# Router logits of a decoder layer: the router's columns stationary in four column groups, the tokens moving

## The chip, the cores and the metric

One core of one Trainium2 chip runs the whole layer in one launch. The metric is device time in microseconds (us), the median of several executions. The kernel before takes 634.29 us (three executions, 633.48 to 638.74).

## What is computed

A decoder layer on 512 tokens of 1024 features: an RMS norm, a combined projection, three groups of heads (differential attention, an RWKV-7 recurrence, cross-attention to a memory), an output projection, and then a mixture of 16 experts. The change lies in the step between the output projection and the experts, the router:

```python
g_logits = xt @ w_gr + b_gr                       # 512 x 4
g_idx = argmax(g_logits)                          # the group of 4 experts
e_logits = (xt @ w_er + b_er).reshape(T, 4, 4)    # 512 x 16
top_v, top_i = top_k(e_logits[rows, g_idx], 2)    # two experts of the group
gate = one_hot(...) * softmax(top_v) * softmax(g_logits)[g_idx]
for e in range(16):
    y += gate[:, e] * (silu(xt @ w_gate[e]) * (xt @ w_up[e])) @ w_down[e]
```

Here `xt` is the normalised row of a token (512 x 1024), and the two router matrices have 4 and 16 columns, kept side by side as 20 columns. The gates decide which tokens an expert gets, so no expert can start before all 512 tokens have been routed.

## The kernel before

The tokens are four tiles of 128 (t0 to t3). The output projection of a tile is made in two halves of 512 columns; the first half is done early for all four, the second half tile by tile (`out_part`, lines L998 to L1000: three float32r products per block, high and low parts of both operands). While one tile is projected, the tiles before it are routed, so that the vector and scalar engines work beside TensorE. The order in which the program names these steps is the string `ORDER`: `a` and `b` are the two quarters of a tile's projection, `x`, `l` and `s` are steps of its routing. The order on each engine is then set by a scheduler that runs a timeline of the whole program in advance and takes, for each engine, what is ready and has the highest priority. Thirty small filler products (`w30`, L1204) have the lowest priority; they stand where TensorE would have nothing else.

`route` does for one tile:

- eight transposes (L1091), four to a PSUM bank, and two ScalarE copies of the banks into `xT` (L1092), which has one buffer for all tiles;
- the logits (L1103): eight float32 products, one per 128 features, summed in PSUM. The stationary operand is a chunk of `xT` (128 features x 128 tokens), the moving one 20 columns of `wr_sb`. Each float32 product runs as two passes on the engine, so a tile has 16;
- on VectorE thirteen small operations from the scaling of the logits (`lgs`, L1105) to `member` (L1121), which marks the two experts of each token;
- one short product with a triangular matrix (L1130), and one with ones for every earlier tile (L1129), to count the members: the rank of each token in its expert (`rankm`, L1131), and a one-hot of the first expert's slots (`ohf`, L1133);
- eight float32 products with that one-hot (L1136, 16 passes) which gather the tokens of expert 0 into the PSUM tile `py`.

After the fourth tile, `py` is split into high and low parts (`xh`, L1267, ScalarE; `xl`, L1269, VectorE), and the products of expert 0 begin (L243 to L245). The weights of the experts arrive on SyncE's queue, and each block of 512 KB is split by ScalarE (`whi`, L96) and VectorE (`wlo`, L97) before it can be used.

The small PSUM tiles of the router come from a pool of two buffers, `pl`, handed out in turn as the program names them: the logits of a tile (`pr_`), then its counts (`pk`), then the next tile's logits.

Of the kernel before, what the change touches and what calls it, by code (L numbers as in the profile page):

```python
# [10 lines left out]
F32 = mybir.dt.float32  # L11
# [3 lines left out]
AF = mybir.ActivationFunctionType  # L15
# [5 lines left out]
P = 128  # L21
# [3 lines left out]
KC = D // P  # L25
# [125 lines left out]
def hybrid_layer_kernel(ctx, tc, x, mem, positions, cols, w_in, w_kv, w_out, wa2, g2, ffn, wr, br,  # L151
                        wg, wu, wd, out):
    nc = tc.nc
    V, A, G, T = nc.vector, nc.scalar, nc.gpsimd, nc.tensor
# [10 lines left out]
    pools = {"ps": psum_ctx.enter_context(tc.tile_pool(name="psa", bufs=2, space=PSUM))}  # L165
# [5 lines left out]
    def pp():  # L171
        return psp.tile([P, 512], F32, name="pp", bufs=4)
# [32 lines left out]
    ident = const.tile([P, P], F32, name="ident")  # L205
# [27 lines left out]
    bones = const.tile([P, P], F32, name="bones")  # L233
# [89 lines left out]
    wr_sb = rc.tile([P, KC, 20], F32, name="wr_sb")  # L323
# [706 lines left out]
    pools["ps"] = ctx.enter_context(tc.tile_pool(name="psl", bufs=2, space=PSUM, reuse_waits="tile"))  # L1030

    def pl(n):
        return pools["ps"].tile([P, 96], F32, name="pl", bufs=2)[:, 0:n]

    gain = rt.tile([P, D], F32, name="gain", bufs=1)
    with later():
# [31 lines left out]
    def first_max(val, mxv, oh):  # L1068
        mi = rt.tile([P, 1], F32, name="fm_i")
        V.tensor_reduce(mxv, val, axis=AX.X, op=ALU.max)  # L1070
        V.scalar_tensor_tensor(oh, val, mxv, rank4, op0=ALU.is_equal, op1=ALU.mult)
        V.tensor_reduce(mi, oh, axis=AX.X, op=ALU.max)
        V.tensor_scalar(oh, oh, mi, -BIG, op0=ALU.not_equal, op1=ALU.mult)
# [7 lines left out]
        (V if i else G).tensor_mul(xns[t][:, c0:c0 + n], x1c, gain[:, c0:c0 + n])  # L1081

    last_act = []

    def route(t, x1):
        tk = slice(t * P, (t + 1) * P)
        xT = rt.tile([P, KC, P], F32, name="xT", bufs=1)
        for b in range(2):
            ps = pp()
            for k in range(4):  # L1090
                T.transpose(ps[:, k * P:(k + 1) * P], x1[:, (b * 4 + k) * P:(b * 4 + k + 1) * P], ident)  # L1091
            last_act.append(A.activation(xT[:, b * 4:b * 4 + 4, :].rearrange("p a b -> p (a b)"), ps, AF.Copy))  # L1092
            if b == 0:
                yield
        yield
        r = rt.tile([P, 1], F32, name="rx1")
        V.tensor_reduce(r, sqs[:, t, :], axis=AX.X, op=ALU.add)
        G.tensor_scalar(r, r, 1.0 / D, RMS_EPS, op0=ALU.mult, op1=ALU.add)
        G.tensor_tensor(r, r, mhalf, op=ALU.pow)
        yield  # L1100
        pr_ = pl(32)
        for k in range(KC):
            T.matmul(pr_[:, 0:20], xT[:, k, :], wr_sb[:, k, :], start=k == 0, stop=k == KC - 1)  # L1103
        lg = lgs[:, t, :]
        V.scalar_tensor_tensor(lg, pr_[:, 0:20], r, br_sb, op0=ALU.mult, op1=ALU.add)  # L1105
        goh = rt.tile([P, 4], F32, name="goh")
        first_max(lg[:, 0:4], tops[:, 0, t:t + 1], goh)
        el = rt.tile([P, 4, 4], F32, name="el")
        V.tensor_add(el, lg[:, 4:20].rearrange("p (a b) -> p a b", a=4), goh[:, :, None].to_broadcast([P, 4, 4]))
        elf = el.rearrange("p a b -> p (a b)")  # L1110
        best = rt.tile([P, 8], F32, name="best")
        where = rt.tile([P, 8], mybir.dt.uint32, name="where")
        wheref = rt.tile([P, 2], F32, name="wheref")
        V.max(best, elf)
        V.max_index(where, best, elf)
        V.tensor_copy(wheref, where[:, 0:2])
        V.tensor_tensor(hots[:, :, t, :], iota16[:, None, :].to_broadcast([P, 2, NE]),
                        wheref[:, :, None].to_broadcast([P, 2, NE]), op=ALU.is_equal)
        V.tensor_copy(tops[:, 1:3, t], best[:, 0:2])
        oh1, oh2 = hots[:, 0, t, :], hots[:, 1, t, :]  # L1120
        V.tensor_add(member[:, t, :], oh1, oh2)  # L1121
        xn = xns[t]
        last_act.append(A.activation(xn, xn, AF.Copy, scale=r))
        nc.scalar.dma_start(xn_d[tk, :], xn)
        nc.sync.dma_start(out[tk, :], x1)
        yield
        pk = pl(32)
        for u in range(t):
            T.matmul(pk[:, 0:NE], onb, member[:, u, :], start=u == 0, stop=False)  # L1129
        T.matmul(pk[:, 0:NE], tri, member[:, t, :], start=t == 0, stop=True)  # L1130
        V.scalar_tensor_tensor(rankm[:, t, :], pk[:, 0:NE], 1.0, member[:, t, :], op0=ALU.add, op1=ALU.mult)  # L1131
        ohf = rt.tile([P, CAP], F32, name="ohf", bufs=4)
        V.tensor_scalar(ohf, slot1, rankm[:, t, 0:1], None, op0=ALU.is_equal)  # L1133
        yield
        for k in range(KC):
            T.matmul(first_py[:, k // 4, (k % 4) * CAP:(k % 4 + 1) * CAP], xn[:, k * P:(k + 1) * P], ohf,  # L1136
                     start=t == 0 and k % 4 == 0, stop=t == NT - 1, skip_group_check=True)
        yield
# [30 lines left out]
    first_py = pools["ps"].tile([P, 2, 512], F32, name="py", bufs=1)  # L1169
    pss = {}  # L1170
    turns = [route(t, x1s[t]) for t in range(NT)]

    def step(t, n=1):
# [65 lines left out]
    def table(e0, e1, w=6):  # L1239
        ps = pl(96)  # L1240
        values = slot_rows(ps, e1 - e0, [rankm[:, t, e0:e1] for t in range(NT)], [rhs[:, t, e0:e1, :] for t in range(NT)],
                           slot1, w)
        tab = ps[0:CAP, 0:(e1 - e0) * 6].rearrange("p (e k) -> p e k", k=6)
        got_idx.append(slot_index(tab, slice(e0, e1)))

        def rest():
            if w < 6:
                values()
            slot_rest(tab, slice(e0, e1))
        return rest  # L1250
# [120 lines left out]
    with tc.If(full > CAP):  # L1371
        with tc.For_i(0, NE, 1) as e:
# [5 lines left out]
            for b in range(1, (S + CAP - 1) // CAP):  # L1378
                base = ex_p.tile([P, CAP], F32, name="base")
                V.tensor_scalar(base, slot1, float(b * CAP), None, op0=ALU.add)  # L1380
                ps = pl(96)
# [56 lines left out]
```

## Time and profile before

| what | value |
|---|---|
| median of three executions | 634.29 us |
| lowest, highest | 633.48, 638.74 us |
| the profiled execution | 633.17 us, its span 631.4 us |
| TensorE busy | 600.7 us (95% of the span) |
| VectorE, ScalarE busy | 498.0 us (79%), 413.0 us (65%) |
| the last product of the projection starts | 316.0 us |
| the first product of expert 0 starts | 332.07 us |

The span is what the trace covers; the 1.8 us between it and the profiled execution's time lie outside of it. Of the 631.4 us some 25 belong to the second halves of the projection and the routing beside them, 16 to the end of the routing, and 299 to the experts.

### The profile page before, as it was taken

To read this page: it belongs to the slowest core of one execution; us is meant where nothing else is said; L and a number is where in the kernel's file an instruction comes from. 1 tells how busy PE (TensorE), PEld (TensorE's weight loads), DVE (VectorE), ACT (ScalarE), POOL (GpSimd) and SP (SyncE) were. 2 spreads that over 40 slices of the span, in tenths; PEclk is the share of its full clock that TensorE was granted. 3 is DMA by queue.
4 is the path that set the end of the run, shared out by engine and by line. 5 is a ranking of instruction groups with operands and counts; after the bars stand their busy time and mean duration, and the time that the engine had idled before them with its cause. 6 is when DMAs were issued, how large, how long until landed. Compare 5 with 4: busy or idle time off the path is not lost.

```text
span 631.4 us, 10888 instructions
## 1 busy us (share of the span) xinstructions
PE 600.7 (95%) x3986; PEld 482.1 (76%) x3986; DVE 498.0 (79%) x893; ACT 413.0 (65%) x622; POOL 126.3 (20%) x129
## 2 busy tenths in 40 slices
PE   3899999999999999999998999999999999999992
PEld 3777879999998877889996777777777777777771
DVE  5854996699755778555468999999999999988991
ACT  3677344544367766655247788888889888888880
POOL 6802010335400114304001011111011111310001
PEclk9999989999999999999999999999999999999997
DMA  8523233333432030889789999999999999799813
GB/s 304 158 79 87 80 102 83 101 95 108 103 83 68 2 134 1 292 278 344 274 315 310 354 348 370 369 372 356 360 357 363 364 366 373 227 379 374 320 25 54
DMA packets 77501, 144.17 MB, mean 228 GB/s; under 512 B 12832, under 2 KB 30496, under 8 KB 77440
## 3 DMA queue, kind: packets, MB, share of 16 engines
q1 hardware_dynamic: 69200, 126.07, 56.9%
q0 software_dynamic: 3760, 13.24, 8.9%
q10 hardware_dynamic: 4480, 4.09, 2.1%
q8 instruction: 33, 0.54, 0.4%
q14 instruction: 28, 0.23, 0.1%
HBM read 131.72 MB, written 11.67 MB: 227 GB/s over the span
## 4 chain that ended last, share of the span: by engine, by line
PE 86%; DVE 6%; ACT 3%; DMA 2%; issue 1%; POOL 1%; POOLq 0%; ACTq 0%; DVEq 0%
PE pp L243 16%; PE pp L245 16%; PE pp L244 16%; PE py L244 5%; PE py L245 4%; PE py L243 4%; PE pp L998 2%; PE pp L999 2%; PE pp L1000 2%; PE pt L921 2%; PE pp L1280 1%; PE py L1136 1%; PE pc L781 1%; DVE wlo L97 1%; PE pl L1103 1%
## 5 line engine op out<-in xcount | busy, mean ns | idle before, releaser
L245 PE MATMUL pp<-whi,xl 128*96 128x512 f32 x264 | 104.0, 395 | 0.0
L244 PE MATMUL pp<-wlo,xh 128*96 128x512 f32 x264 | 103.8, 394 | 0.0
L243 PE MATMUL pp<-whi,xh 128*96 128x512 f32 x264 | 101.2, 394 | 0.8 <-ACT xh L1267 0.8
L1328 POOL DMA_INDIRECT out<-ye,sidx x16 | 23.2, 1452 | 226.0 <-DVE gidx L1230 90.7
L97 DVE TENSOR_TENSOR wlo<-raw,whi 128x1024 fp32r<-128x1024 f32 x42 | 52.3, 1258 | 15.5 <-ACT whi L96 15.0
L96 ACT ACTIVATE whi<-raw 128x1024 fp32r<-128x1024 f32 x42 | 44.1, 1059 | 31.2 <-PE pp L245 14.0
L243 PE MATMUL pp<-whi,hm_h 128*128 128x256 f32 x224 | 63.5, 284 | 0.1
L245 PE MATMUL pp<-whi,hm_l 128*128 128x256 f32 x224 | 63.3, 283 | 0.0
L244 PE MATMUL pp<-wlo,hm_h 128*128 128x256 f32 x224 | 63.1, 282 | 0.0
L243 PEld LDWEIGHTS pp<-whi,xh 128*96 128x96 f32 x264 | 42.5, 161 | 19.6 <-ACT xh L1267 1.3
L245 PEld LDWEIGHTS pp<-whi,xl 128*96 128x96 f32 x264 | 42.6, 161 | 18.4
L244 PEld LDWEIGHTS pp<-wlo,xh 128*96 128x96 f32 x264 | 42.5, 161 | 18.2
L244 PE MATMUL py<-wlo,hh 128*96 128x512 f32 x120 | 47.9, 399 | 0.0
L245 PE MATMUL py<-whi,hl 128*96 128x512 f32 x120 | 47.1, 392 | 0.0
L243 PE MATMUL py<-whi,hh 128*96 128x512 f32 x120 | 47.0, 392 | 0.0
L97 DVE TENSOR_TENSOR wlo<-u,whi 128x1024 fp32r<-128x1024 f32 x34 | 40.8, 1224 | 6.3 <-ACT whi L96 6.3
L97 DVE TENSOR_TENSOR wlo<-lraw,whi 128x1024 fp32r<-128x1024 f32 x36 | 42.6, 1218 | 2.8 <-ACT whi L96 2.7
L243 PEld LDWEIGHTS pp<-whi,hm_h 128*128 128x128 f32 x224 | 42.0, 188 | 2.0 <-issue 0.7
L245 PEld LDWEIGHTS pp<-whi,hm_l 128*128 128x128 f32 x224 | 42.1, 188 | 0.6 <-issue 0.2
L244 PEld LDWEIGHTS pp<-wlo,hm_h 128*128 128x128 f32 x224 | 42.1, 188 | 0.5 <-issue 0.2
L96 ACT ACTIVATE whi<-lraw 128x1024 fp32r<-128x1024 f32 x36 | 37.1, 1059 | 5.1 <-PE pp L245 3.6
L96 ACT ACTIVATE whi<-u 128x1024 fp32r<-128x1024 f32 x34 | 35.2, 1058 | 6.7 <-PE pp L1000 3.7
(397 smaller groups left out, 1545.5 us busy)
## 6 DMA issues: line engine op xcount, KB each, us to landing
raw<-in_w_in SPq DMA_DIRECT2D x22, 512.0 KB, 3.8
u<-in_wd SPq DMA_DIRECT2D x12, 512.0 KB, 7.3
lraw<-in_wg SPq DMA_DIRECT2D x12, 512.0 KB, 11.7
lraw<-in_wu SPq DMA_DIRECT2D x12, 512.0 KB, 9.3
lraw<-in_wd SPq DMA_DIRECT2D x12, 512.0 KB, 12.5
f<-in_wg SPq DMA_DIRECT2D x11, 512.0 KB, 10.3
u<-in_wu SPq DMA_DIRECT2D x11, 512.0 KB, 12.5
eraw<-in_wd SPq DMA_DIRECT2D x10, 512.0 KB, 13.4
```

Of the source, the lines that this page charges most:

```text
L96: nc.scalar.activation(hi, slot, AF.Copy)
L97: nc.vector.tensor_sub(lo, slot, hi.bitcast(F32))
L243: T.matmul(ps, ah, bh, start=first, stop=False)
L244: T.matmul(ps, ah, bl, start=False, stop=False)
L245: T.matmul(ps, al, bh, start=False, stop=last)
L781: T.matmul(px[:, h * C:(h + 1) * C], u1[:, q, ci, h], sav[:, c, h, :], start=h == 0, stop=True, skip_group_check=True)
L921: T.matmul(po[:, 0:P], aws[i % 2][:, kb * P:(kb + 1) * P], qk["v"][:, kb, h * P:(h + 1) * P], start=kb == 0, stop=kb == qb)
L998: T.matmul(o, ah, hi[:, k % 4, :], start=k == k0 and i == lead, stop=False, skip_group_check=True)
L999: T.matmul(o, ah, lo[:, k % 4, :], start=False, stop=False, skip_group_check=True)
L1000: T.matmul(o, al, hi[:, k % 4, :], start=False, stop=k == k1, skip_group_check=True)
L1103: T.matmul(pr_[:, 0:20], xT[:, k, :], wr_sb[:, k, :], start=k == 0, stop=k == KC - 1)
L1328: G.indirect_dma_start(out, bass.IndirectOffsetOnAxis(ap=si, axis=0), ye, None, compute_op=ALU.add)
```

## The change

The roles of the operands are exchanged. A chunk of the router's columns is stationary (32 columns: its own 20 and the first 12 of the next chunk, which are left unused; 20 columns for the last chunk), and the 128 features x 128 tokens of `xT` move. Chunk k writes 32 rows of the PSUM tile `pq` that begin at row 32 x (k mod 4): the four chunks of a half stand in four column groups of the array, and the second half adds to the first. ScalarE copies `pq` over the first chunk of `xT` (L1115 of the changed kernel), and one float32 product with a matrix of ones and zeros, `fold`, sums the four groups and turns the result, so that the logits stand as before (L1117). `fold` is built once by three additions on the first columns of `bones`, a constant of an earlier stage. The pool `pl` gets buffers of 128 columns, and `pq` is one more tile taken from it.

```diff
-        return pools["ps"].tile([P, 96], F32, name="pl", bufs=2)[:, 0:n]
+        return pools["ps"].tile([P, 128], F32, name="pl", bufs=2)[:, 0:n]
...
+    wr_f = wr_sb.rearrange("p a b -> p (a b)")
+    fold = bones[:, 0:20]
+    V.tensor_add(fold, ident[:, 0:20], ident[:, 32:52])
+    V.tensor_add(fold, fold, ident[:, 64:84])
+    V.tensor_add(fold, fold, ident[:, 96:116])
...
+        pq = pl(P)
+        before = None
+        for k in range(KC):
+            w0 = (k % 4) * 32
+            n = 20 if k == KC - 1 else 32
+            with nullcontext() if before is None else tc.issue_after(before.ins):
+                before = T.matmul(pq[w0:w0 + n, :], wr_f[:, k * 20:k * 20 + n], xT[:, k, :], start=k < 4, stop=k >= 4,
+                                  skip_group_check=True)
+        lt = xT[:, 0, :]
+        A.activation(lt, pq, AF.Copy)
         pr_ = pl(32)
-        for k in range(KC):
-            T.matmul(pr_[:, 0:20], xT[:, k, :], wr_sb[:, k, :], start=k == 0, stop=k == KC - 1)
+        T.matmul(pr_[:, 0:20], lt, fold, start=True, stop=True)
```

The scheduler answers with another order. Behind the change the lines are 5 to 14 higher: L1091 is L1096, L1103 is L1112 (and L1117 the fold), L1123 is L1137, L1129 and L1130 are L1143 and L1144, L1136 is L1150, L1204 is L1218. In the rows, `u` holds the tile's residual rows, `pp` is a PSUM bank, `pl` the router's PSUM tiles, `whi` and `wlo` the split weights, `hm_h` and `hm_l` the split input of the projection.

On TensorE, at the end of the second projection half of t2, the logits of t1 and the first transposes of t2 stand like this before:

```order
L1000 MATMUL pp<-xhi_3142,hm_l 128x256
L1091 MATMUL pp<-ident,u_2360 128x128 x2
L1103 MATMUL pl<-wr_sb,xT 128x20
L1091 MATMUL pp<-ident,u_2360 128x128
L1103 MATMUL pl<-wr_sb,xT 128x20
L1091 MATMUL pp<-ident,u_2360 128x128
L1103 MATMUL pl<-wr_sb,xT 128x20 x2
L998 MATMUL pp<-whi_85,hm_h 128x256
```

and now:

```order
L1000 MATMUL pp<-xhi_3142,hm_l 128x256
L1112 MATMUL pl<-xT,wr_sb 32x128 x4
L1096 MATMUL pp<-ident,u_2360 128x128
L1112 MATMUL pl<-xT,wr_sb 32x128
L1096 MATMUL pp<-ident,u_2360 128x128
L1112 MATMUL pl<-xT,wr_sb 32x128
L1096 MATMUL pp<-ident,u_2360 128x128
L1112 MATMUL pl<-xT,wr_sb 32x128
L1096 MATMUL pp<-ident,u_2360 128x128
L1112 MATMUL pl<-xT,wr_sb 20x128
L998 MATMUL pp<-whi_85,hm_h 128x256
```

All eight products of t1 stand there, the first four together and the last four one by one between full-width transposes.

On TensorE, at the end of the routing (the second half of t2's logits, the fillers, the logits of t3, the gathers L1136), before:

```order
L1103 MATMUL pl<-wr_sb,xT 128x20 x4
L1136 MATMUL py<-ohf,xg 128x96 x8
L1129 LDWEIGHTS onb
L1129 MATMUL pl<-member,onb 128x16
...
L1204 MATMUL pp<-onb 128x128
L1103 MATMUL pl<-wr_sb,xT 128x20 x8
L1204 LDWEIGHTS onb
```

and now:

```order
L1112 MATMUL pl<-xT,wr_sb 20x128
L1218 LDWEIGHTS onb
L1218 MATMUL pp<-onb 128x128
...
L1150 MATMUL py<-ohf,xg 128x96 x3
L1117 MATMUL pl<-bones,xT 128x20
L1150 MATMUL py<-ohf,xg 128x96 x5
...
L1112 MATMUL pl<-xT,wr_sb 32x128 x7
L1112 MATMUL pl<-xT,wr_sb 20x128
L1144 LDWEIGHTS tri
L1144 MATMUL pl<-member,tri 128x16
L1117 MATMUL pl<-bones,xT 128x20
```

All thirty fillers and three gathers of t1 now stand ahead of t2's fold, and t3's logits and fold behind it; before, nine fillers and eight gathers stood between the logits of t2 and those of t3.

On ScalarE at the same place, before and now:

```order
L1123 ACTIVATE xg<-xg,rx_3604 128x1024
L1124 DMA xn_d<-xg 128x1024
L1092 ACTIVATE xT<-pp 128x512 x2
L96 ACTIVATE whi_85<-f_2367 128x1024
L96 ACTIVATE whi_87<-f_2367 128x1024
L1146 ACTIVATE gex<-gex 128x16
```

```order
L1137 ACTIVATE xg<-xg,rx_3616 128x1024
L1115 ACTIVATE xT<-pl 128x128
L1138 DMA xn_d<-xg 128x1024
L1097 ACTIVATE xT<-pp 128x512
L1097 ACTIVATE xT<-pp 128x512
L96 ACTIVATE whi_85<-f_2367 128x1024
L96 ACTIVATE whi_87<-f_2367 128x1024
L1115 ACTIVATE xT<-pl 128x128
```

The copy of t2's `pq` is put ahead of t3's two copies into `xT`, and the copy of t3's `pq` behind two splits of expert weights.

## Rows read from the trace of the kernel before

**Rows 1.** The profile's page: shares of the span in the chain that ended last.

```profile
PE 86%; DVE 6%; ACT 3%; DMA 2%; issue 1%; POOL 1%; POOLq 0%; ACTq 0%; DVEq 0%
```

**Rows 2.** One line, L1103: durations (ns, min/median/max), first and last start (us).

```profile
L1103 PE MATMUL pl<-wr_sb,xT x64: 180/266/266, 293.9 to 324.9; 128*128 128x20 f32 x64
```

**Rows 3.** The chain of waits, 284 to 345 us: start, duration, what.

```profile
320.22 0.80 PE pl L1103 x8
321.02 1.85 PE py L1136 x16
322.91 0.52 PE pp L1204 x9
323.42 1.75 PE pl L1103 x16
325.17 0.45 PE pp L1204 x8
325.64 0.74 PE pp L1204 x13
...
329.49 2.01 PE py L1136 x16
...
332.07 0.48 PE pp L243
```

**Rows 4.** The timeline of TensorE at 258 us: start, duration, what, count.

```profile
258.33 0.28 PE L1000 MATMUL pp<-whi,hm_l 128*128 128x256 f32 x1
258.44 0.28 PE L998 MATMUL pp<-whi,hm_h 128*128 128x256 f32 x1
258.65 0.44 PE L945 MATMUL pt<-aw,mv 128*64 128x256 f32 x2
258.92 0.39 PE L945 MATMUL pt<-aw,mv 128*64 128x256 f32 x2
259.23 0.39 PE L999 MATMUL pp<-wlo,hm_h 128*128 128x256 f32 x1
259.45 0.28 PE L1000 MATMUL pp<-whi,hm_l 128*128 128x256 f32 x1
```

**Rows 5.** The chain of waits at 110 us: a float32 product with 512 columns.

```profile
110.31 0.86 PE pc L628 x2
```

**Rows 6.** The timeline of VectorE, 321 to 329 us.

```profile
321.13 0.24 DVE L1105 SCALAR_TENSOR_TENSOR lgs<-pl,rx,br_sb 128x20 f32<-128x20 f32 x1 [2.72 <-PE pl L1103]
...
323.44 0.17 DVE L1121 TENSOR_TENSOR member<-hots 128x16 bf16<-128x16 f32 x1
325.28 0.24 DVE L1105 SCALAR_TENSOR_TENSOR lgs<-pl,rx,br_sb 128x20 f32<-128x20 f32 x1 [1.66 <-PE pl L1103]
...
328.24 0.17 DVE L1121 TENSOR_TENSOR member<-hots 128x16 bf16<-128x16 f32 x1
...
329.08 0.27 DVE L1133 TENSOR_SCALAR ohf<-slot,rankm 128x96 f32<-128x96 f32 x1
```

**Rows 7.** The timeline of ScalarE, 321 to 327 us.

```profile
321.06 1.08 ACT L1092 ACTIVATE xT<-pp 128x512 f32<-128x512 f32 x2 [0.56 <-PE pl L1103]
322.03 2.00 ACT L96 ACTIVATE whi<-f 128x1024 fp32r<-128x1024 f32 x2
326.12 0.22 ACT L1146 ACTIVATE gex<-gex 128x16 f32<-128x16 f32 x1 [2.09 <-DVE gex L1144]
```

**Rows 8.** Busy time by stretch: PE, PEld, DVE, ACT, POOL, granted clock, DMA share, GB/s.

```profile
80.00:83.60 3.60, 2.15 (x12) 1.23 (x11) 3.55 (x6) 1.92 (x3) 0.00 (x0) 1.00 0.02 5
83.60:87.05 3.45, 3.36 (x18) 3.13 (x19) 3.42 (x6) 0.76 (x2) 0.01 (x1) 0.51 0.17 41
350.00:600.00 250.00, 250.00 (x1231) 178.93 (x1230) 235.29 (x331) 206.87 (x238) 36.89 (x26) 1.00 1.01 352
```

**Rows 9.** The timeline of VectorE, 112 to 119 us: where the additions for `fold` now stand.

```profile
118.68 0.09 DVE L675 MEMSET r_t<- 128x32 f32 x1 [5.11 <-DMA r_t<-ud_d]
```

**Rows 10.** Waits, 330 to 632 us: the longest of ScalarE for a weight transfer.

```profile
ACT whi L96 <- DMA qT<-in_wd: 0.3, 1, 0.3
```

## The prediction

> **What bounds the kernel now.** I began with the chain that ended last: 86% of it is TensorE [rows 1], so what a change does to TensorE's order of work is what counts. Then I read that chain around the router [rows 3]. The reader is to see two regimes there. Up to 321 us TensorE never pauses: projection, transposes and logits follow each other, and every microsecond of router work is a microsecond of the kernel. From 321 us on the fillers stand in the chain (0.52 + 0.45 + 0.74 = 1.71 us for thirty): TensorE now waits for the routing of the last tile, and the latency counts: logits of t3, thirteen VectorE operations, the count, the one-hot, the gather (329.49), the first expert product (332.07). From there TensorE is full again: busy 250.00 of 250 us between 350 and 600 us [rows 8], and the longest wait of ScalarE for a weight transfer is 0.3 us [rows 10]. So the experts give nothing back: a later start of expert 0 is a later end.
>
> **Prices.** A pass of the logits costs 1.75/16 = 0.11 us, from sixteen in a row [rows 3]; 64 passes [rows 2] make 7.0 us, four quarters of 1.75. In the new form the moving side has 128 columns. The nearest float32 product with a wide moving side takes 0.43 us per pass of 512 columns [rows 5], hence 0.107 us for 128. A pass alone is therefore no cheaper than before; the gain must come from column groups that work at the same time.
>
> Two such groups are in the trace, the memory attention's products L945 [rows 4]. They come in pairs, two rows that start together (258.65, then 258.92). From the product at 258.44 to the one at 259.45 are 1.01 us. In it lie two ordinary products of 0.11 (the step from 258.33 to 258.44) and two pairs at 0.21 (256 columns at the price of rows 5), 0.64 together. Two groups do overlap fully, and the way into this mode and out of it costs the remaining 0.36 us.
>
> Four groups are in no row. Lower bound: all four overlap, and four products (eight passes) cost 0.36 + 2 x 0.107 = 0.58 us against 8 x 0.11 = 0.88. Upper bound: one after the other, 0.36 + 8 x 0.107 = 1.22. I take the lower one, since rows 4 show two groups without any loss. One product that stands alone between full-width work costs 0.36 + 0.21 = 0.57 us against 0.22, in either case. The fold is two passes like the old ones, 0.22.
>
> **TensorE up to the end of t2's logits**, by the new order:
> - t0: two groups of four, -0.60, a fold, +0.22: -0.38.
> - t1: one group of four, -0.30. The other four stand singly between transposes: 4 x 0.57 - 0.88 = +1.40. A fold, +0.22. Together +1.32.
> - t2: one single, a three, a four: 0.57 + 0.58 + 0.58 = 1.73 against 1.75: nothing.
>
> That is +0.9 us: t2's logits, which ended at 321.02 [rows 3], end near 321.95. The new waits inside this stretch have cover: folds of t0 and t1 stand some 22 projection products (2.5 us) behind their logits, and the ScalarE copy between takes 0.22 to 0.60 us (a 16-column and, per copy, 512-column operation, [rows 7]); I take 0.3 for 128 columns. If that cover were gone, each fold would hold TensorE by some 0.5 us.
>
> **The end of the routing.** Here lies the larger term. `lt` is written over `xT`, so t3's copies into `xT` must wait for t2's fold, and that fold stands behind all thirty fillers and three gathers. 321.95 + 1.71 (fillers) + 0.70 (six of sixteen passes in 1.85 us) = 324.35; the fold ends at 324.6, t2's `lgs` starts at 324.75. Before, it started at 321.13 [rows 6]: 3.6 us later. Then two paths run side by side to t3's fold:
> - ScalarE: t3's copies 324.7 to 325.8, then two weight splits queued ahead of t3's `pq` copy. In the old rows [rows 7] copies and splits take 321.06 to 324.03, 2.97 us; so they end at 327.7, and the copy at 328.0. t3's logits (0.36 + 0.43 us) are done by 326.6 and cost nothing.
> - VectorE: from `lgs` to the end of `member` 2.48 us [rows 6], to 327.25. Then the count and `rankm`, which must free the second buffer of `pl` before t3's fold may write it. From the end of t3's `member` (328.41) to the end of `ohf` (329.35) passed 0.94 us, 0.27 of it `ohf` itself; I take 0.65: 327.9.
>
> Both say 328.0. The fold takes 0.22, and with the 0.1 us that the old `lgs` followed its last pass, t3's `lgs` starts near 328.35 instead of 325.28: +3.1. From `lgs` to the end of `ohf` the old tile t3 took 4.07 us with t2's one-hots between; these are now ahead of it, while three gate operations move ahead of `rankm` and `ohf`. I count +0.5 (three operations of about 0.2 added, less what leaves the chain; bounds -0.4 and +0.8). The gather of sixteen passes is unchanged, and the short count products that now stand ahead of expert 0 were behind its second product before. Expert 0 starts 3.6 us later.
>
> Costs at nothing: three additions on VectorE at 113 us, ahead of an idle 5.11 us that ends with a transfer [rows 9]; without this gap they would cost some 0.6 us. Queues: no transfer on SyncE's or GpSimd's queue is added, and t2's and t3's normalised rows go out on ScalarE's queue ahead of the late folds, well before the first gather from memory. At the end of the kernel a split or two changes place among full buffers: 0 to +0.4.
>
> **Sum.** 633.17 + 3.6 = 636.8 us against the profiled execution. This one was 1.1 us below the median of the runs shown, so on the median: 634.29 + 3.6 = **637.9 us**, 0.6% more. One per cent, 6.3 us, is about what a measurement of this kernel can tell from no change.
>
> **Rivals.**
> 1. *The exchange pays.* If no fold held anything up, 7.0 us of passes would shrink to a quarter, 1.75, plus four folds of 0.88: -4.4, 629.9 us. For it: rows 4, groups do overlap. Against it: the 0.36 us per change of mode, and the fillers ahead of t2's fold. The Trainium skill (TensorEngine Tiling (Array Packing), Performance Considerations) recommends just this exchange where the moving side is 32 wide or less, with a factor of up to 4. By that rule the sum would be this rival's; the rows say that the passes are only 7 us and that the latency behind them is dearer. 7 in 100.
> 2. *The tail gives it back.* t2's late fold is partly hidden: fillers run shorter when real work is ready, or the two paths to t3's fold are a microsecond shorter each. Then +0.5 to +2: about 635.5. 15 in 100.
> 3. *The groups do not overlap*, one column group after the other. t0: 2 x 0.34 + 0.22 = +0.90. t1: +0.34 + 1.40 + 0.22 = +1.96. t2: 0.57 + 1.00 + 1.22 - 1.75 = +1.04. Together +3.9 instead of +0.9, all of it ahead of t2's fold: 637.9 + 3.0 = 640.9 us, slower by over 1%. It decides as soon as a group of four costs 1.2 us rather than 0.58. For it: four groups read four moving streams of float32 at once, which no row shows. Against it: rows 4. 15 in 100.
> 4. *The clock falls at the end of the routing.* In 80 to 83.6 us TensorE was busy 2.15 of 3.60 us, and the next 3.45 us ran at a granted 0.51, about 1.2 GHz [rows 8]; 3.36 us of busy time at half rate cost some 1.7 us. The new tail leaves TensorE idle for some 3 of 9 us, where the fillers no longer help. 637.9 + 1.7 = 639.6 us. 18 in 100.
>
> The forecast itself keeps 45 in 100. The range from 635.0 to 641.3 takes in rivals 2 to 4 and the bounds of +0.5; outside are the first rival, the lower edge of the second, and rivals 3 and 4 together. Faster by over 1% would need more than rival 1 gives: 0.02. Slower by over 1% (above 640.6) is most of rival 3 and a corner of rival 4: 0.14. Within 1%: 0.84.
>
> **What would show it.** In the profile after: rows of four column groups that start together with a step near 0.11 us between rounds (else rival 3); t1's logits and the transposes among them over 2.5 us or more; the chain at 322 to 325 us through fillers, L1150 and the fold L1117; t3's `xT` copies begin only after that fold, and its `pq` copy after two `whi`; `lgs` of t3 near 328.3 and the first product of expert 0 near 335.7; the distance from there to the end as before, 299 us; a granted clock of 1.00 in the stretch 325 to 340 us (else rival 4). The forecast is wrong if t2's fold runs before the fillers do, or if expert 0 starts late and the end does not move.

## The result, and the profile after

| | before | after |
|---|---|---|
| median of the runs | 634.25 us (632.81 to 638.74, 10 runs) | 641.07 us (640.20 to 641.77, 10 runs) |
| ratio, 95% interval | | 1.0096 (1.0078 to 1.0115) |
| profiled execution, span | 633.17 us, 631.4 us | 641.05 us, 639.2 us |
| mean granted clock of that execution | 0.991 | 0.980 |
| first product of expert 0, in the chain | 332.07 us | 339.54 us |

The change costs 6.8 us by the medians, 1.1%; 3.6 us were forecast. The time lies inside the range, at its upper edge. Two runs took far longer than the others of their kernel and are left out here and below: 682.43 us, one of 60 further runs of the kernel before, and 646.87 us, one of six of `late_fill`.

The page of the kernel after: the chain's shares, for [rows 1], and the granted clock in forty slices of 16 us.

```profile
PEclk9999989999999997999997999999999999999997
PE 87%; DVE 5%; ACT 3%; issue 1%; POOL 1%; DMA 1%; POOLq 0%; DVEq 0%; ACTq 0%
```

The bound is the same. What is new are the two 7s inside the clock row. Busy time by stretch, kernel after, for [rows 8] (PE, PEld, DVE, ACT, POOL, granted clock, DMA share, GB/s):

```profile
244.80:251.60 6.80, 6.68 (x31) 5.73 (x32) 6.11 (x13) 2.34 (x9) 2.85 (x2) 0.50 0.01 2
330.00:337.00 7.00, 4.75 (x49) 4.38 (x49) 6.21 (x34) 1.41 (x4) 0.00 (x0) 1.00 0.98 345
337.00:343.90 6.90, 6.65 (x35) 5.14 (x35) 4.91 (x12) 1.93 (x3) 2.98 (x3) 0.51 0.45 133
350.00:600.00 250.00, 248.73 (x1223) 177.59 (x1222) 235.01 (x333) 205.80 (x239) 35.43 (x25) 1.00 1.03 357
```

The same stretch in the kernel before ran 55 products instead of 31, at full clock:

```profile
244.80:251.60 6.80, 5.97 (x55) 5.25 (x54) 5.79 (x10) 2.39 (x8) 2.86 (x2) 1.00 0.01 2
```

So twice, at 245 us and at 337 us, TensorE ran for 6.8 us at the lower level, 1.2 GHz. The first time is 50 us ahead of the router's first transposes. From 350 us on TensorE is full, as before.

The logits and the transposes among them: the timeline of TensorE, kernel after, for [rows 4] (start, duration, what, count, idle time before and what ended it).

```profile
297.47 0.66 PE L1096 MATMUL pp<-ident,u 128*128 128x128 f32 x4 [0.43 <-DVE u L1077]
...
301.23 0.42 PE L1112 MATMUL pl<-xT,wr_sb 128*32 128x128 f32 x8
...
301.80 0.28 PE L999 MATMUL pp<-wlo,hm_h 128*128 128x256 f32 x1
...
304.54 0.28 PE L1000 MATMUL pp<-whi,hm_l 128*128 128x256 f32 x1
305.60 0.66 PE L1096 MATMUL pp<-ident,u 128*128 128x128 f32 x4 [0.79 <-DVE tops L1070]
...
312.15 0.33 PE L1096 MATMUL pp<-ident,u 128*128 128x128 f32 x1
312.41 0.41 PE L1112 MATMUL pl<-xT,wr_sb 128*32 128x128 f32 x2
312.74 0.33 PE L1096 MATMUL pp<-ident,u 128*128 128x128 f32 x1
```

The row at 301.23 holds eight passes of four products, and all of them start before 301.58, where the projection goes on: the four column groups do work at once. A transpose that alternates with a single product takes a step of 0.60 us with it (312.15 to 312.74); 0.11 of it is the transpose, 0.49 the product. And twice the transposes waited, 0.43 and 0.79 us, for `u` (L1077), the VectorE operation that makes their input; the row at 305.60 names `tops`, the next operation on VectorE. That was not in the forecast. TensorE and VectorE at the second place, before:

```profile
302.06 0.28 PE L1000 MATMUL pp<-whi,hm_l 128*128 128x256 f32 x1
302.21 1.05 PE L1103 MATMUL pl<-wr_sb,xT 128*128 128x20 f32 x8
302.37 0.69 DVE L1077 TENSOR_TENSOR u<-pp,u 128x512 f32<-128x512 f32 x1 [0.26 <-PE pl L1130]
303.12 0.66 PE L1091 MATMUL pp<-ident,u 128*128 128x128 f32 x4
```

ScalarE and VectorE there, kernel after; the last two rows are later ones, for what follows:

```profile
304.53 0.60 ACT L1097 ACTIVATE xT<-pp 128x512 f32<-128x512 f32 x1 [2.52 <-PE pl L1117]
304.61 0.24 DVE L1119 SCALAR_TENSOR_TENSOR lgs<-pl,rx,br_sb 128x20 f32<-128x20 f32 x1 [5.62 <-PE pl L1117]
304.85 0.69 DVE L1077 TENSOR_TENSOR u<-pp,u 128x512 f32<-128x512 f32 x1
...
317.54 0.24 DVE L1119 SCALAR_TENSOR_TENSOR lgs<-pl,rx,br_sb 128x20 f32<-128x20 f32 x1 [5.61 <-PE pl L1117]
...
335.00 0.26 DVE L1147 TENSOR_SCALAR ohf<-slot,rankm 128x96 f32<-128x96 f32 x1
```

VectorE stands idle for 5.62 us until t0's fold, and `u` of t1 stands behind the `lgs` that waits for it. This looks like the cause of the wait and is not: `u` starts 0.31 us behind the last product of its projection now (304.54 to 304.85) and before (302.06 to 302.37), and the transposes start 1.06 us behind that product now (305.60) and before (303.12). At t0 these are 1.06 us in both kernels too (293.79 to 294.85, 296.41 to 297.47). What has changed is what stands in them. Before, it was four logits products each time. Now t0's four are shorter, and t1's four are gone to 311.79: their input is copied into `xT`, and this copy now waits for t0's fold (304.53; before it started at 299.54).

t1's `lgs` starts 7.04 us later than before (310.50): 2.6 of these the whole program is late by then, 1.7 are its longer logits, and 2.8 the fold, which stands that much further behind them. From there to its one-hot it loses 2.6 more, most of it to other work of VectorE in between (from `lgs` to the end of `member` 4.93 us, 2.48 before); the one-hot is 9.7 us late (325.65 against 315.99).

The chain of waits behind t2's logits, kernel after, for [rows 3] (start, duration, what):

```profile
324.80 0.35 PE pl L1112 x7
325.15 0.22 PE pp L1218 x2
325.38 1.58 PE pp L1218 x28
326.96 0.70 PE py L1150 x6
327.66 0.17 PE pl L1117 x2
327.92 0.25 DVE lgs L1119
...
331.55 0.25 DVE lgs L1119
...
335.08 0.19 DVE ohf L1147
...
335.41 2.27 PE py L1150 x16
338.17 1.37 PE pl L1239 x16
339.54 0.58 PE pp L243
340.12 0.43 PE pp L244
```

Fillers, three gathers (six passes), the fold, `lgs`: the order of the forecast. At the foot, the low clock: an expert product takes 0.43 us. ScalarE beside it, for [rows 7]:

```profile
327.85 1.08 ACT L1097 ACTIVATE xT<-pp 128x512 f32<-128x512 f32 x2 [2.35 <-PE pl L1117]
328.82 2.00 ACT L96 ACTIVATE whi<-f 128x1024 fp32r<-128x1024 f32 x2
330.72 0.28 ACT L1115 ACTIVATE xT<-pl 128x128 f32<-128x128 f32 x1
```

t3's copies did wait for t2's fold, and t3's `pq` copy for two splits behind them.

The 7.8 us between the two spans, cut at places that both traces have:

| stretch | before | after | more | forecast |
|---|---|---|---|---|
| start to a product of L884 ahead of the first fall | 243.66 | 244.01 | 0.35 | 0 |
| to the first transpose of t0 | 292.20 | 294.82 | 2.27 | 0 |
| to the end of t2's logits | 321.02 | 325.15 | 1.51 | 0.9 |
| to t3's gather | 329.49 | 335.41 | 1.79 | 2.7 |
| to the first expert product | 332.07 | 339.54 | 1.55 | 0 |
| to the last product on TensorE | 618.78 | 627.72 | 1.47 | 0 |
| to the end of the span | 631.4 | 639.2 | -1.14 | 0 to 0.4 |

### The profile page after: what moved, and what is told of

It is laid out like the page before. It is cut to its first block, busy times and chain, and to the rows that moved or that the text cites. A ratio compares the mean times of both kernels' runs of the same rounds, so it can differ in the third digit from the quotient of the medians.

```text
span 639.2 us, 10916 instructions
## 1 busy us (share of the span) xinstructions
PE 607.3 (95%) x3994; PEld 483.2 (76%) x3994; DVE 497.6 (78%) x896; ACT 413.5 (65%) x626; POOL 125.4 (20%) x129
## 4 chain that ended last, share of the span: by engine, by line
PE 87%; DVE 5%; ACT 3%; issue 1%; POOL 1%; DMA 1%; POOLq 0%; DVEq 0%; ACTq 0%
PE pp L243 16%; PE pp L245 16%; PE pp L244 16%; PE py L244 4%; PE py L245 4%; PE py L243 4%; PE pp L998 3%; PE pp L999 2%; PE pp L1000 2%; PE pt L921 2%; PE pp L1294 1%; PE pc L781 1%; PE pp L884 1%; DVE wlo L97 1%; ACT whi L96 1%
## 5 line engine op out<-in xcount | busy, mean ns | idle before, releaser
L243 PE MATMUL pp<-whi,xh 128*96 128x512 f32 x264 | 102.7, 398 | 0.4 <-ACT xh L1281 0.4
```

The lines of the kernel that those rows point to most:

```text
L243: T.matmul(ps, ah, bh, start=first, stop=False)
```

## The experiments

Two theories. **A:** the router's own terms cost about what was forecast, and the rest, some 4 us, is the two stretches of low clock. **B:** the rest is the new form too, in waits that were not priced. Each run is compared with runs of the kernel before on the same chip. Those spread from 631.5 to 638.5 us, and go with the mean granted clock: a straight line through all 59 falls by 0.40 us per 0.001 of clock and reads 637.4 us at 0.980. The last column of the table is the median distance of a kernel's runs from this line, at their own clock. It is a rough measure, since what a low stretch costs depends on its place.

| kernel | median us | ratio (95%) | median clock | off the line |
|---|---|---|---|---|
| after | 641.07 | 1.0078 to 1.0115 | 0.980 | +3.6 |
| `old_adds` | 634.15 | 0.9984 to 1.0036 | 0.988 | +0.1 |
| `old_hold` | 634.94 | 0.9993 to 1.0041 | 0.987 | +0.2 |
| `hold` | 635.37 | 1.0011 to 1.0069 | 0.988 | +1.8 |
| `grouped` | 638.25 | 1.0045 to 1.0110 | 0.979 | +0.5 |
| `both` | 635.11 | 1.0005 to 1.0053 | 0.986 | +0.2 |
| `first_two` | 640.33 | 1.0076 to 1.0157 | 0.981 | +3.7 |
| `last_two` | 636.85 | 1.0025 to 1.0083 | 0.984 | +1.3 |
| `no_fill` | 641.23 | 1.0099 to 1.0160 | 0.981 | +4.0 |
| `late_fill` | 639.38 (637.10 to 640.06, 5 runs) | 1.0051 to 1.0107 | 0.987 | +4.8 |

### The three additions alone (`old_adds`)

The kernel before, with the new lines that make `fold`; nothing reads it.

```diff
+    fold = bones[:, 0:20]
+    V.tensor_add(fold, ident[:, 0:20], ident[:, 32:52])
+    V.tensor_add(fold, fold, ident[:, 64:84])
+    V.tensor_add(fold, fold, ident[:, 96:116])
```

> The kernel before with nothing added but the three additions that build the fold matrix (it is not used); TensorE's order is that of before. Theory A, that everything the change costs comes from the router's own work and waits and from TensorE's idle time in it: no change, 634.3 us (633.5 to 635), granted clock 1.00 around 245 us as before. Rival, that the fall of the clock at 245 us in the changed kernel, ahead of any router work, comes from any small change of the program: about 1.9 us more, 636.2, with a stretch at half clock near 245 us.

634.15 us, as before; the first expert product stands at 332.07 us, and there is no low clock at 245 us in the trace. The additions cost nothing that can be told from these runs, as forecast [rows 9], and don't bring on the fall by themselves.

### The fillers tied to three places (`hold`)

The thirty low-priority fillers are taken out; others are tied to a place behind t2's logits, t3's logits and t3's count. The fourteen of the first place still stand ahead of t2's fold, here and in `both`, whose expectation says that none does.

```diff
-... x3 s0 s1 s2 l3 s2 s3 s3 w30"
+... x3 s0 s1 s2 l3 s2 s3 s3"
+    def filler(after, n):
+        bank = pp()
+        with tc.issue_after(after.ins):
+            for _ in range(n):
+                T.matmul(bank[:, 0:128], onb, onb[:, 0:128], start=True, stop=True)
...
+        if t >= NT - 2:
+            filler(before, 14)
         lt = xT[:, 0, :]
...
+        if t == NT - 1:
+            filler(counted, 18)
```

> The changed kernel with the thirty free fillers replaced by 14 behind t2's logits, 14 behind t3's logits and 18 behind t3's count, where TensorE stood idle (0.9, 0.4 and 1.1 us). Theory A: the second fall of the clock (337 to 344 us) comes from that idle time; with it filled the granted clock stays 1.00 there, the first products of expert 0 take 0.23 us instead of 0.43, and the kernel gains about 2.2 us: 638.9 against 641.1. Rival, that the clock falls there whatever TensorE does: 641, and the products at 0.43 us.

635.37 us, 5.7 less than the kernel after, where theory A had 2.2. In this order t2's fold stands ahead of t1's gathers. The chain of `hold`:

```profile
322.68 0.69 PE pp L1094 x12
323.37 0.19 PE pl L1127 x2
...
323.60 1.86 PE py L1162 x16
...
331.58 1.81 PE py L1162 x16
...
333.96 0.84 PE pl L1251 x16
334.81 0.31 PE pp L243
```

The fold runs 1.8 us after the end of t2's logits (321.57) instead of 2.5. From the first transpose to the first expert product `hold` takes 42.7 us (292.12 to 334.81), the kernel after 44.7 us (294.82 to 339.54), the kernel before 39.9 us (292.20 to 332.07). So some 2 us of the 5.7 are the routing; the rest is that neither stretch of low clock is in this trace. At full clock the way from t3's gather to the first product is 3.23 us, against 2.58 before [rows 3] and 4.13 after: that is how the table's 1.55 us divide into 0.65 for the sixteen short products that now stand ahead of expert 0 and 0.90 for the clock. The 0.65 us are no loss. In the kernel before these products stand behind expert 0's second product:

```profile
332.61 0.84 PE L1225 MATMUL pl<-rhs,ohs 128*96 128x3 bf16 x16
```

From the first expert product to the last product on TensorE are 286.71 us before and 285.74 in `hold`, at full clock in both traces. So 0.97 us come back there, and the table's 1.47 us are 2.44 of clock less these 0.97.

### The same fillers in the old form (`old_hold`)

The same edit in the kernel before: 14 fillers behind t2's logits, 14 behind t3's, 18 behind t3's count.

> The old form of the logits with the fillers spread in the same manner (14 behind t2's logits, 14 behind t3's, 18 behind t3's count), a control for the run with the new form and spread fillers. Theory A (in the old form the fillers hold nothing up, since t3's logits stand ahead of them, so placing them otherwise moves nothing): 634.2 us within 0.7. Theory B (the spread fillers themselves are worth something, by a clock that stays up or gathers that start earlier, whatever the form of the logits): 632.5 us or less, and then the gain of spreading in the new form is no sign that the late fold was the cost.

634.94 us, at the upper edge of theory A of this run; the interval holds no change. Spread fillers are worth nothing where no fold stands behind them, so what `hold` gains in the routing is not theirs.

### No fillers at all (`no_fill`)

The kernel after without `w30` in `ORDER`.

> The changed kernel without any filler product. The prediction put 1.71 us of fillers on the path to t2's fold. Theory A (they stand there only beside a wait: the gathers behind them need the one-hots of t1, which came at 325.9 us in the changed kernel, so without fillers TensorE is idle instead): t2's fold still near 327.3 us, the time 641.0 us within 0.8 as long as the clock falls no longer than it did, up to 643.5 if it falls for 13 us. Theory B (they are on the path, as predicted): t2's fold 1.7 us earlier, near 325.8 us, and 639.3 us.

641.23 us, and t2's fold is no earlier. The chain of `no_fill`:

```profile
324.94 0.13 PE pl L1144
...
325.31 0.28 DVE ohf L1147
...
325.72 2.00 PE py L1150 x16
327.72 0.17 PE pl L1117 x2
```

Where the fillers stood, TensorE now waits for t1's one-hot (`ohf`) and then runs t1's gathers, all sixteen passes, ahead of the fold. The forecast read the fillers as the price. They only lay beside the price: t1's routing, late since its single products and its fold.

### t1's products together (`grouped`)

The next tile's transposes wait for the last product of the tile before.

```diff
+            with tc.issue_after(ended[t - 1].ins) if t and b == 0 else nullcontext():
                 for k in range(4):
                     T.transpose(...)
...
+        ended[t] = before
         lt = xT[:, 0, :]
```

> The changed kernel with each tile's first transposes held behind the last logits product of the tile before, so that the four products of t1 that stood singly stand together. Theory A: five changes of the array's mode become one; t1's eight products take 0.7 us instead of 2.7, about 2 us less for TensorE ahead of t2: 639 against 641.1. Rival, that single products cost nothing since TensorE has slack there (its transposes waited 0.4 and 0.8 us for VectorE): 641.

638.25 us. The timelines of TensorE and VectorE of `grouped`:

```profile
311.78 0.64 PE L1115 MATMUL pl<-xT,wr_sb 128*32 128x128 f32 x16
312.36 0.66 PE L1099 MATMUL pp<-ident,u 128*128 128x128 f32 x4
312.77 0.37 PE L998 MATMUL pp<-whi,hm_h 128*128 128x256 f32 x1
...
331.86 0.27 DVE L1151 TENSOR_SCALAR ohf<-slot,rankm 128x96 f32<-128x96 f32 x1
```

Eight products and four transposes take 0.99 us here (311.78 to 312.77); in the kernel after 2.73 us (311.79 to 314.52). Both stretches of low clock are still there (245.0 and 333.8 us, 6.8 us each), so most of the 2.8 us come from the router's order.

How much the order is worth shows at a place that the clock has not reached yet, the start of t3's one-hot, counted from the first transpose of t0; the clock is at its full level between the two in all seven traces:

| kernel | first transpose | t3's one-hot | distance |
|---|---|---|---|
| before | 292.20 | 329.08 | 36.9 |
| after | 294.82 | 335.00 | 40.2 |
| `no_fill` | 294.61 | 335.32 | 40.7 |
| `hold` | 292.12 | 330.80 | 38.7 |
| `grouped` | 294.86 | 331.86 | 37.0 |
| `both` | 293.86 | 330.70 | 36.8 |
| `old_hold` | 297.41 | 334.35 | 36.9 |

Putting t1's products together takes away all but 0.1 us of the 3.3 us that the routing loses up to there; the order of `hold` takes away 1.5, and only 0.2 more once the products stand together. Products that stand alone in their mode, with what they delay, are the dearest item of the new form.

### Both mends (`both`)

The edits of `hold` and `grouped` together.

> All four tiles in the new form, with both mends at once: the products of a tile stand together (the next tile's transposes wait for them), and the fillers are spread so that none stands ahead of t2's fold. Theory A (the two costs lie in different places, one ahead of the end of t2's logits, one behind it, and add up): the spread fillers alone gave 635.4 us, the grouping alone took 2.8 us off the changed kernel, of which some 2 us without a part that the clock decides; so 633.4 us, between 632.7 and 634.2, level with the kernel before, with the first expert product near 332.7 us in the trace. Theory B (behind the end of t2's logits the latency of the routing is the bound, and what TensorE saves ahead of it is waited for there): 635.4 us as with the spread fillers alone, first expert product near 334.7 us. If the clock falls once more (about 6.8 us at half rate), 2 us more in either case.

635.11 us, in twelve runs from 631.66 to 638.75. By its time theory B; by its trace theory A: the first expert product comes 40.7 us behind the first transpose (293.86 to 334.57), 0.8 us more than in the kernel before. Its profiled execution came to the routing 1.7 us late, with low clock at 83 us (6.8 us, in the kernel before 3.4) and again at 247 us. At the same granted clock of 0.994 the two best runs, 631.66 and 632.19 us, lie where four of the kernel before do (631.73 to 632.13). By its interval the mended new form is 0.05 to 0.5% slower than the old one, by the line 0.2 us: level, or a little behind. It does not beat it.

### The new form for two tiles (`first_two`, `last_two`)

```diff
-        pq = pl(P)
-        ...
+        if t < 2:      # last_two: t > 1
+            pq = pl(P)
+            ...
+        else:
+            pr_ = pl(32)
+            for k in range(KC):
+                T.matmul(pr_[:, 0:20], xT[:, k, :], wr_sb[:, k, :], start=k == 0, stop=k == KC - 1)
```

> The new logits for the tiles t0 and t1, the old form for t2 and t3. Theory A: the stretch of TensorE up to the end of the projection is about 2 us longer as in the changed kernel (t1's single products and two waits of transposes for VectorE), the end of the routing is as before, and the clock does not fall at the end of the routing: 636.2 us, or 638 if the clock falls at 245 us. Rival, that the end of the routing alone makes the loss: 634.5.

> The new form for t2 and t3 alone, the old one for t0 and t1. Theory A (the terms of the parts add up): TensorE reaches the end of t2's logits as in the kernel before, near 321.1 us; t2's fold stands behind fillers and gathers, so the routing ends some 3.5 us later than before: first expert product near 335.5 us, 637.5 us; 639.5 us if the clock falls at the end of the routing as in the changed kernel. Theory B (the late fold of t2 costs little, and it is t0's and t1's waits and the clock that made the changed kernel slow): at most 635.5 us, first expert product near 333.5 us.

`first_two` took 640.33 us, a miss by 4 us; `last_two` 636.85 us, near theory A's 637.5, but its runs go from 634.65 to 641.50 us, and its trace has a fall, for which theory A had 639.5. Busy time by stretch of `first_two`:

```profile
320.00:329.60 9.60, 9.60 (x111) 9.50 (x111) 4.63 (x26) 4.45 (x8) 0.74 (x2) 1.00 1.01 367
329.60:343.30 13.70, 12.78 (x66) 11.06 (x66) 9.49 (x36) 2.35 (x5) 2.99 (x3) 0.50 0.59 191
```

and of `last_two`:

```profile
328.70:342.40 13.70, 12.21 (x66) 10.21 (x65) 9.29 (x32) 2.31 (x5) 2.99 (x3) 0.50 0.67 213
```

In both the clock is low for 13.7 us, twice as long as in the kernel after, and neither has the fall at 245 us. The parts don't add up to the whole; what the clock takes differs from kernel to kernel by as much as the parts. That `first_two` was busy for all of the 9.6 us ahead also speaks against the reason that rival 4 gave, TensorE's idle time.

### Fillers in the idle places of the tail (`late_fill`)

The kernel after, with its thirty fillers, and 14 more behind t3's logits and 18 behind t3's count.

> The changed kernel with its thirty fillers, and 14 more fillers behind t3's logits and 18 behind t3's count, where TensorE stood idle for some 3 us of 9. The order of the routing is that of the changed kernel: t2's fold still behind the gathers, t2's logits scaled near 327.9 us. Theory A (of what the changed kernel lost, about 2.2 us is the lower clock behind the routing, and TensorE's idle time ahead of it brings that on): with the idle time filled the granted clock stays at 1.00 from 330 to 345 us, the first expert product comes near 338.5 us and the time is 638.9 us, between 638 and 639.7. Theory B (the idle time is not what brings the clock down, or the fillers themselves now stand in the way of the count and the gather): the clock falls as before or the gain is eaten, 641 us or more.

639.38 us, the number of theory A and the course of theory B. The clock fell all the same, and sooner. Busy time by stretch of `late_fill`:

```profile
320.00:330.00 10.00, 8.05 (x83) 6.77 (x83) 5.76 (x32) 4.79 (x8) 0.04 (x1) 0.87 1.00 355
330.00:337.00 7.00, 7.00 (x59) 7.00 (x59) 3.65 (x18) 0.20 (x1) 0.00 (x0) 0.50 0.42 152
```

Its gain came from elsewhere: no low clock at 84 us or at 245 us, and so 3.9 us of lead at the first transpose (290.88 against 294.82). The tail was 4.8 us longer than in the kernel after (290.88 to 340.38, 49.5 us to the first expert product instead of 44.7), with fillers and gathers at half rate. Filling idle time there was no remedy.

## Why the prediction was right, and where it was short

- **Four groups at once: right.** A block of four products took 0.55 us with its changes of mode (from the last transpose ahead of it, 301.03, to the product at 301.80 are 0.77 us, less two ordinary products of 0.11); 0.58 were taken from [rows 4, 5], rival 3 needed 1.2. The Trainium skill (TensorEngine Tiling (Array Packing), Key Properties) says that a change of mode drains the engine; the rows give the price, 0.27 us more for a product alone (0.49) than in the old form (0.22).
- **t1's singles: right, a little too dear.** Forecast 0.57 each, measured 0.49. What they delay was not priced; `grouped` shows the whole item.
- **"Every microsecond of router work is a microsecond of the kernel": the step that failed.** The stretch up to the end of t2's logits cost 1.51 us, 0.9 were forecast. Four products of t0 and four of t1 had stood in the 1.06 us in which the transposes wait for `u` anyway. There a shorter form saves nothing: up to t1's last projection product t0 came to -0.14 us (9.86 us before, 292.20 to 302.06; 9.72 after, 294.82 to 304.54), not to -0.38. And t1's four, moved out of this place, are added in full: from its second transposes to the projection behind its logits are 8.92 us (305.60 to 314.52), 7.12 before (303.12 to 310.24). That is +1.80, and with its fold some +1.9, where +1.32 were forecast. t2 gave 0.2 back. That the folds have cover on TensorE was right. But t0's fold holds `xT`, and so it moves t1's four products.
- **t2's fold: the right moment for the wrong reason.** From the end of t2's logits to `lgs` 2.8 us were forecast and 2.77 measured. But without fillers it is no less (`no_fill`): t1's late one-hot holds the gathers, and the gathers hold the fold. With t1's products together the whole loss is gone (`grouped`).
- **Two paths to t3's fold: right.** From t2's `lgs` to t3's 3.60 us forecast, 3.63 measured, with `pq`'s copy behind two splits, as the forecast had it.
- **From t3's `lgs` to its one-hot: wrong sign.** +0.5 forecast, -0.36 measured (3.71 us from 331.55 to the end of `ohf` at 335.26; 4.07 before [rows 6]). The bounds were -0.4 to +0.8: what left the chain was worth more than the gate operations that came in. Rival 2 looked for its gain in the fillers and in the two paths, and there was none in either.
- **Short products ahead of expert 0: taken as nothing, right in the sum.** They cost 0.65 us ahead of it at full clock and give 0.97 back behind it (`hold`).
- **Sum of the router's terms** at full clock: 1.51 + 1.79 + 0.65 - 0.97 = 2.98 us, 3.6 forecast. The errors of single terms, up to 0.9, partly cancel, and that is luck. Off the line of the kernel before, the ten runs give +3.6.
- **Rival 4, the clock: right that it falls behind the routing, wrong in size and reason.** 18 in 100 and 1.7 us were given to one fall. Measured: 0.90 + 2.44 us behind the routing, and 2.27 us at 245 us, where no router work stands and no term had one; 5.6 us in all in the profiled execution. With the router's 3.0, the 0.35 us ahead of both and less the 1.14 us that the end of the kernel gave back, for a reason that was not looked for, these are its 7.8 us. On the medians, where the kernel before has low stretches in many runs too (median clock 0.988, the profiled execution 0.991), the difference is 6.8. So the forecast's own mechanism accounts for some 3 to 3.6 of the 6.8 us and the clock for the rest; the time lies inside the range because that was drawn wide enough for rival 4.
- **The exchange pays (rival 1): refuted for the orders that were tried.** The best of them, `both`, is level with the old form, not 4.4 us faster. No run has the new form without any wait.

**Open:** what brings the clock down. The fall at 245 us is in the traces of the kernel after, `grouped` and `no_fill`, and a little later (246.7) in `both`. It is not in those of the kernel before, `old_adds`, `hold`, `first_two`, `last_two` and `late_fill`, although the work ahead of it on TensorE is the same, in the same order, in all (`old_hold` has one at 208 us). Each trace is one run. The fall behind the routing is in every trace with the new form except `hold` and `both`. All ten runs of the kernel after have a mean clock of 0.977 to 0.982, so there it is no chance of one run; the runs of `both` go from 0.981 to 0.994. No run here takes the fall at 245 us away and leaves the rest of the kernel after as it is.

## What to carry to other kernels

Before an exchange of the stationary and the moving operand, price the product that stands alone in its mode (here 0.49 against 0.22 us) and the extra step of the chain, not the pass, and put the products of a tile together: here that alone took away the routing's loss. Look also at what a product fills. One that stands in a wait is free: shortened, it saves nothing; moved elsewhere, it is added in full. Where an engine is idle ahead of an operation that matters, look first when that operation's own input was ready: `u` stood behind an idle VectorE and was not late. And compare runs at their granted clock before a difference of under 1% is given to the edit.

## What was not expected of the hardware

- Four float32 column groups run fully side by side: 64 passes in the new form, and a round of four products with 128 columns each in some 0.13 us (the second round of t0's first block starts at 296.75, the first at 296.62).
- The same kernel takes from 631.5 us (mean granted clock 0.993) to 638.5 us (0.981). It can stay at half for 13.7 us of work in which TensorE is 12.8 us busy, right behind 9.6 us without a pause (`first_two`).
